# Scan states of a head pair: stored without zero blocks, and each head's states and queries multiplied in their own corner of the array

## The chip, the cores and the metric

The kernel runs on one core of one Trainium2 chip. The metric is the device time of one execution in microseconds (us), as the median of several runs. The engines named below are PE (TensorE, the matrix array), PEld (its weight loads), DVE (VectorE), ACT (ScalarE), POOL (GpSimd) and SP (which issues most DMAs).

## The reference, cut to what matters

Two trunk layers work on 256 context tokens and 1024 latent tokens of width 1024. Each has a mixing part and an MLP. The mixing part has four groups of four heads (HGRN2, mLSTM, retention, GLA). Each group runs a forward and a backward chunkwise scan and sums the two.

```python
def step(S, inp):                       # chunk_linear: HGRN2, retention, GLA
    qc, kc, vc, ac = inp
    b = jnp.cumsum(ac, axis=-2)
...
    b_last = b[..., -1:, :]
    o = (jnp.einsum('bhts,bhsv->bhtv', attn, vc)
         + jnp.einsum('bhtk,bhkv->bhtv', qc * jnp.exp(b), S))
    S_new = (jnp.exp(b_last[..., 0, :])[..., None] * S
             + jnp.einsum('bhsk,bhsv->bhkv', kc * jnp.exp(b_last - b), vc))
    return S_new, o
```

A state S has dk rows (64 for HGRN2 and retention, 32 for GLA) and dv = 64 columns for each head. The change touches the second term of o (queries times state) and the place where S_new is kept. The mLSTM scan has a form of its own (chunk_mlstm), whose states the kernel keeps in another buffer.

## The kernel before, in words

All 1280 tokens lie as 10 chunks of 128 columns; channels lie on the partitions. One layer runs: norm and modulation; the mixers; the output projection; the MLP. All dense products are made of three matmuls each (L294 to L296, or L632 to L634 for values, L601 for GLA's values and the small gates), with operands split into a high and a low part in a type that PE takes in one pass. The scans' matmuls are plain f32, and the trace shows each of them as two matmul records (two passes), each with its own weight load.

In `mixers` the scans run one after another: GLA (four heads at once), HGRN2 pair 0 and 1, mLSTM pair 0 and 1, retention pair 0 and 1. Each scan is a generator; the class `Fill` lets dense products of the projections and gates run between its steps, so that PE has work while DVE and ACT prepare the scan's operands. The order that results in each engine's queue is made when the program is built: a scheduler moves instructions that are ready ahead of others, so an instruction may stand far from its neighbours in the source.

A scan (`mix_vec` for GLA and HGRN2, `mix_rt` for retention) has two parts.

- The states. For 4, 4 and 2 chunks the keys are transposed, `state_update` (L818) multiplies keys and values of each head into one PSUM bank, and `evac_states` copies the results into the buffer ST on ACT. ST has 128 columns for each chunk and direction: rows of the pair's first head have their state in columns 0 to 63 and zeros in 64 to 127, rows of the second head the other way round. To get the zeros each bank is copied twice with a 0/1 column as scale (`hsel`, L1196). mLSTM calls the same function without a scale (L1193). Then `chain` runs the recurrence over the chunks on DVE: eight dependent instructions for each direction (L799 and L803), 16 for each scan.
- The outputs. For up to 4 chunks the queries are scaled (L919, L1038), the attention matrix is built over levels of halved blocks (L976 to L1032, on DVE, ACT and PE), `direct` makes its innermost two diagonals (L932 to L959, with a small matmul on L956), and `out_chunks` sums everything in a PSUM bank: for each direction one matmul of ST with the queries (L831), then for each head one matmul of the values with the attention matrix (L834), which fills half of the array's columns, at column 0 or 64. `finish` (L703 to L710) normalises.

The buffers of the scans come from `Heap`, a next-fit allocator; the size of ST's buffer is in `SIZES`.

Of the kernel before, what the change touches and what calls it, by code (L numbers as in the profile page):

```python
# [9 lines left out]
AF = mybir.ActivationFunctionType  # L10
# [6 lines left out]
NC = 10  # L17
# [180 lines left out]
class K:  # L198
# [346 lines left out]
        self.late = (tb, r)  # L545


    SIZES = {"raw": NC * 48, "V": NC * 256, "V65": NC * 260, "S": NC * 256, "S65": NC * 130}

    def get(self, S, name):  # L550
        if name not in S:
# [269 lines left out]

    def out_chunks(self, chunks, pair, qd, ST, at, V, kt):

        nc = self.nc
        ps = self.bank(self.obank.next())
        r0, kd, vh = pair
        for i, c in enumerate(chunks):
            o = ps[:, 128 * i:128 * i + 128]
            ds = [d for d in range(2) if (c, d) not in ((0, 0), (1, 1))]
            for j, d in enumerate(ds):  # L830
                nc.tensor.matmul(o, lhsT=ST[r0:r0 + kd, c, d, :], rhs=qd[d](c)[r0:r0 + kd, :], start=(j == 0), stop=False,  # L831
                                 tile_position=(r0, 0))
            for h in range(2):
                nc.tensor.matmul(o[64 * h:64 * h + 64, :], lhsT=V[:, c, vh + h, :], rhs=at(vh + h, c), start=False, stop=True,  # L834
                                 tile_position=(0, 64 * h))
        self.finish(kt, ps[:, 0:128 * len(chunks)], chunks[0], len(chunks))


    def mix_vec(self, S, kind):
        nc, hp = self.nc, self.heap  # L840
# [21 lines left out]
        for d in range(2):  # L862
# [3 lines left out]
            nc.vector.tensor_tensor(rs[d][:, :, far], t[:, :, 0], t[:, :, 1], op=ALU.add)  # L866
            nc.scalar.activation(et[d], t, AF.Exp, scale=esc)
            nc.scalar.activation(dc[d], rs[d][:, :, far], AF.Exp, scale=esc)
        ST = self.get(S, "S")(NC, 2, 128)
        gone = [S[x] for x in (("Q", "B0", "B1") + (("G0", "G1") if hg else ("K",)))]  # L870
        gone2 = [S[x] for x in (("S",) if hg else ("S", "V"))]

        for g0, g1 in ((0, 4), (4, 8), (8, 10)):
            n = 128 * (g1 - g0)
            sl = slice(128 * g0, 128 * g1)
            kk = [hp.alloc(n) for _ in range(2)]
            kno = [hp.alloc(n) for _ in range(2)]
            for d in range(2):
                kd = self.v(kk[d], 2 * (g1 - g0), 64)
                ref = rs[d].rearrange("p a b -> p (a b)")[:, 2 * g0:2 * g1].unsqueeze(2).to_broadcast([128, 2 * (g1 - g0), 64])  # L880
                src = (G[d] if hg else B[d])[:, sl].rearrange("p (a b) -> p a b", b=64)
                if hg:
                    nc.vector.tensor_tensor(kd, src, ref, op=ALU.add)
                else:
                    nc.vector.tensor_tensor(kd, ref, src, op=ALU.subtract)
                kf = self.v(kk[d], n)
                nc.scalar.activation(kf, kf, AF.Exp, scale=esc)
                if not hg:
                    nc.vector.tensor_tensor(kf, kf, Kx[:, sl], op=ALU.mult)
                bk = self.mb.next()  # L890
                T = self.bank(bk).rearrange("p (a b) -> p a b", b=128)
                for i in range(g1 - g0):
                    nc.tensor.transpose(T[:, i, :], kf[:, 128 * i:128 * i + 128], self.ident)
                nc.scalar.activation(self.v(kno[d], n), self.bank(bk)[:, 0:n], AF.Copy)
            bk = self.mb.next()
            for d in range(2):
                kn = self.v(kno[d], g1 - g0, 128)
                for i, c in enumerate(range(g0, g1)):
                    f = self.feeds(c, d)
                    if f is None:  # L900
                        continue
                    ps = self.state_update(c, d, kn[:, i, :], V, heads, ST, bk, d * 4 + i, 64)
            self.evac_states(bk, ST, g0, g1, 64, 4, hs)
            hp.free(*kk, *kno)
            yield (g1 - g0) * (220 + 220 * nh)
        self.chain(ST, lambda c, d: dc[d][:, c:c + 1])
# [3 lines left out]
        for g0 in range(first, NC, step):  # L910
# [139 lines left out]
            hp.free(*qo, ato, cto)  # L1050
            skip = 128 * (g0 if g0 == first and first else 0)
            hp.free_head(skip + n, *gone)
            hp.free_head(2 * (skip + n), *gone2)
            yield m * (430 + 436 * nh)
        hp.free(sm, *gone, *gone2)

    def mgroup(self, nh):

# [59 lines left out]
    def mix_rt(self, S):  # L1118
# [1 line left out]
        heads = [(0, 64, 2 * p), (64, 64, 2 * p + 1)]  # L1120
        V = self.v(S["V"], NC, 4, 64)
        Q, Kx = self.v(S["Q"], NT), self.v(S["K"], NT)
        ST = self.get(S, "S")(NC, 2, 128)
        for g0, g1 in ((0, 4), (4, 8), (8, 10)):
            m = g1 - g0
            n = 128 * m
            bk = self.mb.next()
            for i in range(m):
                nc.tensor.transpose(self.bank(bk)[:, 128 * i:128 * i + 128],
                                    Kx[:, 128 * (g0 + i):128 * (g0 + i) + 128], self.ident)  # L1130
            kno = [hp.alloc(n) for _ in range(2)]
            src = self.bank(bk)[:, 0:n].rearrange("p (c h k) -> p c h k", h=2, k=64)
            for d in range(2):
                sc = self.rtK[:, d, 2 * p:2 * p + 2].unsqueeze(1).unsqueeze(3).to_broadcast([128, m, 2, 64])
                nc.vector.tensor_tensor(self.v(kno[d], n).rearrange("p (c h k) -> p c h k", h=2, k=64), src, sc, op=ALU.mult)
            bk = self.mb.next()
            for d in range(2):
                kn = self.v(kno[d], m, 128)
                for i, c in enumerate(range(g0, g1)):
                    if self.feeds(c, d) is not None:  # L1140
                        self.state_update(c, d, kn[:, i, :], V, heads, ST, bk, d * 4 + i, 64)
            self.evac_states(bk, ST, g0, g1, 64, 4, self.hsel[:, 2:4])
            hp.free(*kno)
            yield m * 900
        self.chain(ST, lambda c, d: self.rtd[:, 8 + 2 * d + p:9 + 2 * d + p])
        first = 0 if l == 0 else 2
        for g0 in range(first, NC, 4):
# [21 lines left out]
            hp.free(*qo, ato)  # L1169
            n += 128 * (first if g0 == first else 0)  # L1170
            hp.free_head(n, S["Q"], S["K"])
            hp.free_head(2 * n, S["S"])
            yield m * 1750
        hp.free(S["S"], S["Q"], S["K"])

    def evac_states(self, bk, ST, g0, g1, w, per, sel=None):

        nc = self.nc
        for d in range(2):
            runs = []  # L1180
            for i, c in enumerate(range(g0, g1)):
                f = self.feeds(c, d)
                if f is None:
                    continue
                if runs and f - c == runs[-1][2] - runs[-1][1] and i == runs[-1][0] + runs[-1][3]:
                    runs[-1][3] += 1
                else:
                    runs.append([i, c, f, 1])
            for i, c, f, m in runs:
                o = (d * per + i) * w  # L1190
                src = self.bank(bk)[:, o:o + m * w].rearrange("p (c v) -> p c v", v=w)
                if sel is None:
                    nc.scalar.activation(ST[:, f:f + m, d, :], src, AF.Copy)  # L1193
                else:
                    for e in range(2):
                        nc.scalar.activation(ST[:, f:f + m, d, 64 * e:64 * e + 64], src, AF.Copy, scale=sel[:, e:e + 1])  # L1196


    def ml_rows(self, sp):
# [541 lines left out]
```

## Time and profile before

| | |
|---|---|
| median of 3 runs | 3275.53 us (3268.72 to 3275.95) |
| profiled execution | 3272.16 us, of which its span is 3270.4 us |
| PE busy | 3189.2 us, 98% of the span |
| DVE, ACT, POOL busy | 2098.0, 1285.5, 11.5 us |
| mean granted TensorE clock | 0.992 of full speed |

The span goes from the first to the last instruction; 1.8 us of the execution's time lie outside it. Busy PE means that some matmul was in the array or on its way through it; matmuls are pipelined, so the time that one costs is read from the distance between starts and not from the length of a record.

### The profile page before, as it was taken

To read this page: it belongs to the slowest core of one execution; us is meant where nothing else is said; L and a number is where in the kernel's file an instruction comes from. 1 tells how busy PE (TensorE), PEld (TensorE's weight loads), DVE (VectorE), ACT (ScalarE), POOL (GpSimd) and SP (SyncE) were. 2 spreads that over 40 slices of the span, in tenths; PEclk is the share of its full clock that TensorE was granted. 3 is DMA by queue.
4 is the path that set the end of the run, shared out by engine and by line. 5 is a ranking of instruction groups with operands and counts; after the bars stand their busy time and mean duration, and the time that the engine had idled before them with its cause. 6 is when DMAs were issued, how large, how long until landed. Compare 5 with 4: busy or idle time off the path is not lost.

```text
span 3270.4 us, 52561 instructions
## 1 busy us (share of the span) xinstructions
PE 3189.2 (98%) x20681; PEld 2612.7 (80%) x20681; DVE 2098.0 (64%) x4333; ACT 1285.5 (39%) x2665; POOL 11.5 (0%) x42
## 2 busy tenths in 40 slices
PE   7999999999999999999999999999999999999998
PEld 4787788877888888888888677788778888888887
DVE  4778887776588845454545586876756555555546
ACT  4666564546332121212122575764544322222222
POOL 0000000000000000000000000000000000000000
PEclk9999899999999999999999999999999999999999
DMA  5115565345157511111111222333324111111111
GB/s 208 60 60 178 180 187 195 117 135 183 57 164 232 161 39 39 39 39 39 39 39 40 78 66 71 118 108 115 94 71 149 58 48 49 46 52 46 52 49 65
DMA packets 181953, 308.20 MB, mean 94 GB/s; under 512 B 21880, under 2 KB 51240, under 8 KB 181448
## 3 DMA queue, kind: packets, MB, share of 16 engines
q1 hardware_dynamic: 180376, 303.02, 28.7%
q8 instruction: 162, 2.65, 0.3%
q10 hardware_dynamic: 1296, 1.81, 0.2%
q14 instruction: 87, 0.71, 0.1%
q0 software_dynamic: 32, 0.01, 0.0%
HBM read 259.11 MB, written 45.65 MB: 93 GB/s over the span
## 4 chain that ended last, share of the span: by engine, by line
PE 84%; DVE 6%; DMA 5%; ACT 3%; issue 1%; SPq 0%; DVEq 0%; ACTq 0%
PE psum L294 22%; PE psum L295 22%; PE psum L296 22%; PE psum L831 2%; PE psum L601 2%; PE psum L632 1%; PE psum L834 1%; PE psum L818 1%; PE psum L634 1%; PE psum L633 1%; PE psum L1019 1%; PE psum L706 1%; DMA ph<-w_adaR 1%; PE psum L1358 1%; DVE px L991 1%
## 5 line engine op out<-in xcount | busy, mean ns | idle before, releaser
L526 DVE SCALAR_TENSOR_TENSOR x<-psum,st,x 128x512 f32<-128x512 f32 (+1 forms) x648 | 440.4, 689 | 204.3 <-PE psum L296 203.8
L282 ACT ACTIVATE pc<-st 128x512 fp32r<-128x512 f32 x256 | 161.3, 632 | 853.5 <-PE psum L295 841.3
L295 PE MATMUL psum<-pc,pc 128*128 128x512 f32 (+1 forms) x1296 | 477.1, 368 | 5.0 <-DVE pc L506 5.0
L294 PE MATMUL psum<-pc,pc 128*128 128x512 f32 (+1 forms) x1296 | 476.3, 368 | 0.0
L296 PE MATMUL psum<-pc,pc 128*128 128x512 f32 (+1 forms) x1296 | 474.9, 366 | 0.0
L294 PE MATMUL psum<-Hhi,pc 128*128 128x512 f32 (+1 forms) x1280 | 471.1, 368 | 1.6 <-ACT pc L282 1.5
L295 PE MATMUL psum<-Hlo,pc 128*128 128x512 f32 (+1 forms) x1280 | 472.0, 369 | 0.1
L296 PE MATMUL psum<-Hhi,pc 128*128 128x512 f32 (+1 forms) x1280 | 470.5, 368 | 0.0
L294 PE MATMUL psum<-Hhi,pw 128*128 128x512 f32 (+1 forms) x1192 | 450.8, 378 | 8.3 <-ACT pw L282 3.9
L296 PE MATMUL psum<-Hhi,pw 128*128 128x512 f32 (+1 forms) x1192 | 447.5, 376 | 0.6 <-DVE pw L283 0.6
L295 PE MATMUL psum<-Hlo,pw 128*128 128x512 f32 (+1 forms) x1192 | 446.5, 375 | 0.0
L505 DVE TENSOR_TENSOR st<-st 128x256 f32<-128x256 f32 (+1 forms) x160 | 101.8, 636 | 301.5 <-ACT pc L504 300.8
L295 PEld LDWEIGHTS psum<-pc,pc 128*128 128x128 f32 x1296 | 245.1, 189 | 47.0 <-DVE pc L506 5.5
L294 PEld LDWEIGHTS psum<-pc,pc 128*128 128x128 f32 x1296 | 245.1, 189 | 44.2 <-DVE x L526 1.3
L296 PEld LDWEIGHTS psum<-pc,pc 128*128 128x128 f32 x1296 | 244.7, 189 | 43.0 <-issue 2.7
L294 PEld LDWEIGHTS psum<-Hhi,pc 128*128 128x128 f32 x1280 | 241.3, 189 | 43.3 <-ACT pc L282 2.4
L295 PEld LDWEIGHTS psum<-Hlo,pc 128*128 128x128 f32 x1280 | 241.3, 189 | 40.9 <-issue 0.5
L283 DVE TENSOR_TENSOR pc<-st,pc 128x512 fp32r<-128x512 f32 x256 | 175.6, 689 | 153.3 <-ACT pc L282 133.4
L296 PEld LDWEIGHTS psum<-Hhi,pc 128*128 128x128 f32 x1280 | 241.1, 188 | 41.0 <-DVE pc L283 0.6
L294 PEld LDWEIGHTS psum<-Hhi,pw 128*128 128x128 f32 x1192 | 227.3, 191 | 54.4 <-issue 9.6
L296 PEld LDWEIGHTS psum<-Hhi,pw 128*128 128x128 f32 x1192 | 227.2, 191 | 39.4 <-issue 2.6
L295 PEld LDWEIGHTS psum<-Hlo,pw 128*128 128x128 f32 x1192 | 227.6, 191 | 37.2 <-issue 2.2
(401 smaller groups left out, 4868.6 us busy)
## 6 DMA issues: line engine op xcount, KB each, us to landing
st<-w_ff SPq DMA_DIRECT2D x256, 256.0 KB
ph<-w_adaR SPq DMA_DIRECT2D x128, 256.0 KB
st<-w_inT SPq DMA_DIRECT2D x96, 256.0 KB
st<-w_adaR SPq DMA_DIRECT2D x74, 256.0 KB
pc<-w_adaR SPq DMA_DIRECT2D x54, 256.0 KB
st<-w_out SPq DMA_DIRECT2D x50, 256.0 KB
d_z<-st SPq DMA_DIRECT2D x40, 256.0 KB
ps<-w_ada SPq DMA_DIRECT2D x32, 256.0 KB
```

Source lines behind the costliest of these rows:

```text
L282: nc.scalar.activation(hi, raw, AF.Copy)
L283: (eng or nc.vector).tensor_tensor(lo, raw, F(hi), op=ALU.subtract)
L294: t.matmul(out, lhsT=w[0], rhs=m[0], start=first, stop=False)
L295: t.matmul(out, lhsT=w[0], rhs=m[1], start=False, stop=False)
L296: t.matmul(out, lhsT=w[1], rhs=m[0], start=False, stop=last)
L505: nc.vector.tensor_tensor(r, r, r, op=ALU.mult)
L526: nc.vector.scalar_tensor_tensor(x, ps, self.mod[:, l, 40 + o, j:j + 1], x, op0=ALU.mult, op1=ALU.add)
L601: t.matmul(ps[:, 0:304], lhsT=h[a], rhs=u[b], start=(k + i == 0), stop=(k == NK - 1 and i == 2))
L632: t.matmul(ps[:, e, :], lhsT=h[0], rhs=u[0], start=(k == 0), stop=False)
L633: t.matmul(ps[:, e, :], lhsT=h[0], rhs=u[1], start=False, stop=False)
L634: t.matmul(ps[:, e, :], lhsT=h[1], rhs=u[0], start=False, stop=(k == NK - 1))
L831: nc.tensor.matmul(o, lhsT=ST[r0:r0 + kd, c, d, :], rhs=qd[d](c)[r0:r0 + kd, :], start=(j == 0), stop=False, tile_position=(r0, 0))
```

## The change

`ST` has 64 columns for each chunk and direction in place of 128: every head's state stands in its own rows, without the zero block. `evac_states` has lost its scale and copies each run of chunks once, for all scans. `out_chunks` makes two matmuls for each direction: head h takes its rows of ST as weights and its rows of the queries, and writes output partitions 64h to 64h + 63, so it stands at row a and column 64h of the array. The buffer of ST is half as large, and what is freed at a time is halved with it.

```diff
-    SIZES = {"raw": NC * 48, "V": NC * 256, "V65": NC * 260, "S": NC * 256, "S65": NC * 130}
+    SIZES = {"raw": NC * 48, "V": NC * 256, "V65": NC * 260, "S": NC * 128, "S65": NC * 130}
@@ out_chunks
             for j, d in enumerate(ds):
-                nc.tensor.matmul(o, lhsT=ST[r0:r0 + kd, c, d, :], rhs=qd[d](c)[r0:r0 + kd, :], start=(j == 0), stop=False,
-                                 tile_position=(r0, 0))
+                for h in range(2):
+                    a = r0 + kd // 2 * h
+                    nc.tensor.matmul(o[64 * h:64 * h + 64, :], lhsT=ST[a:a + kd // 2, c, d, :], rhs=qd[d](c)[a:a + kd // 2, :],
+                                     start=(j == 0), stop=False, tile_position=(a, 64 * h))
@@ mix_vec (mix_rt alike)
-        ST = self.get(S, "S")(NC, 2, 128)
+        ST = self.get(S, "S")(NC, 2, 64)
...
-            self.evac_states(bk, ST, g0, g1, 64, 4, hs)
+            self.evac_states(bk, ST, g0, g1, 64, 4)
...
-            hp.free_head(2 * (skip + n), *gone2)
+            for x, k in gone2:
+                hp.free_head(k * (skip + n), x)
@@ evac_states
-    def evac_states(self, bk, ST, g0, g1, w, per, sel=None):
+    def evac_states(self, bk, ST, g0, g1, w, per):
...
-                if sel is None:
-                    nc.scalar.activation(ST[:, f:f + m, d, :], src, AF.Copy)
-                else:
-                    for e in range(2):
-                        nc.scalar.activation(ST[:, f:f + m, d, 64 * e:64 * e + 64], src, AF.Copy, scale=sel[:, e:e + 1])
+                nc.scalar.activation(ST[:, f:f + m, d, :], src, AF.Copy)
```

The counts of instructions change on two engines: PE has 408 state matmuls in place of 204, and ACT has 112 state copies in place of 192 (160 with a scale and 32 of mLSTM). In the changed kernel L831 is L833, L834 is L836, L956 is L958, L1000 and L1019 are L1002 and L1021, L894 and L887 are L896 and L889, L985 is L987, and L1193 and L1196 are L1195.

The scheduler's order moves too. Three places follow. The first is PE's queue in layer 0 at the end of the first output step of HGRN2 pair 0, where `direct` and `out_chunks` follow each other. Before:

```order
L296 MATMUL psum<-Hhi,pw_0_252 128x512
L294 MATMUL psum<-Hhi,pw_0_252 128x512
L295 MATMUL psum<-Hlo,pw_0_252 128x512
L296 MATMUL psum<-Hhi,pw_0_252 128x512
L956 MATMUL psum<-st,px_0_693 128x2 x8
L294 MATMUL psum<-Hhi,pw_0_252 128x256
L295 MATMUL psum<-Hlo,pw_0_252 128x256
L834 MATMUL psum<-px_0_693,ph_0_256 64x128 x2
L831 MATMUL psum<-px_0_693,ph_0_256 128x128
L834 MATMUL psum<-px_0_693,ph_0_256 64x128 x2
L831 MATMUL psum<-px_0_693,ph_0_256 128x128 x2
L834 MATMUL psum<-px_0_693,ph_0_256 64x128 x2
```

And in the changed kernel at the same place:

```order
L294 MATMUL psum<-Hhi,pw_0_252 128x512
L295 MATMUL psum<-Hlo,pw_0_252 128x512
L296 MATMUL psum<-Hhi,pw_0_252 128x512
L294 MATMUL psum<-Hhi,pw_0_252 128x512
L295 MATMUL psum<-Hlo,pw_0_252 128x512
L296 MATMUL psum<-Hhi,pw_0_252 128x512
L958 MATMUL psum<-st,px_0_693 128x2 x4
L836 MATMUL psum<-px_0_693,ph_0_256 64x128 x2
L833 MATMUL psum<-px_0_693,ph_0_256 64x128 x2
L836 MATMUL psum<-px_0_693,ph_0_256 64x128 x2
L833 MATMUL psum<-px_0_693,ph_0_256 64x128 x4
L836 MATMUL psum<-px_0_693,ph_0_256 64x128 x2
```

The eight small matmuls of `direct` stood together before; now the first four stand 13 dense matmuls of 512 columns ahead of the last four (six of the 13 are shown), and the two dense matmuls that stood between `direct` and `out_chunks` are gone from there.

The second is PE's queue a little earlier, at the head of that same output step, where the first state matmul of the pair was moved ahead, among dense matmuls. Before:

```order
L1000 MATMUL psum<-px_0_693 64x64 x14
L296 MATMUL psum<-Hhi,pw_0_252 128x512
L831 MATMUL psum<-px_0_693,ph_0_256 128x128
L1019 MATMUL psum<-px_0_693 32x2x32 x16
L294 MATMUL psum<-Hhi,pw_0_252 128x512
```

And in the changed kernel:

```order
L294 MATMUL psum<-Hhi,pw_0_252 128x512
L833 MATMUL psum<-px_0_693,ph_0_256 64x128 x2
L295 MATMUL psum<-Hlo,pw_0_252 128x512
L296 MATMUL psum<-Hhi,pw_0_252 128x512
L1021 MATMUL psum<-px_0_693 32x2x32 x16
```

The state matmul still stands alone there, now as two, with dense matmuls on both of its sides.

The third is ACT's queue during the states of HGRN2 pair 0 of layer 0, from the first state copies to the scaling of the queries (L918, now L920). Before:

```order
L1196 ACTIVATE ph_0_256<-psum,st 128x4x64 x2
L1196 ACTIVATE ph_0_256<-psum,st 128x64 x6
L894 ACTIVATE px_0_693<-psum 128x512
L887 ACTIVATE px_0_693<-px_0_693 128x512
L887 ACTIVATE px_0_693<-px_0_693 128x256 x2
L308 ACTIVATE st<-st 128x512
L894 ACTIVATE px_0_693<-psum 128x512
L894 ACTIVATE px_0_693<-psum 128x256 x2
L918 ACTIVATE px_0_693<-ph_0_256 128x512
L1196 ACTIVATE ph_0_256<-psum,st 128x4x64 x4
L1196 ACTIVATE ph_0_256<-psum,st 128x64 x2
L1196 ACTIVATE ph_0_256<-psum,st 128x2x64 x2
```

And in the changed kernel:

```order
L1195 ACTIVATE ph_0_256<-psum 128x64
L708 ACTIVATE st<-st 128x128
L896 ACTIVATE px_0_693<-psum 128x512 x2
L308 ACTIVATE st<-st 128x512
L889 ACTIVATE px_0_693<-px_0_693 128x256 x2
L309 ACTIVATE st<-st 128x512
L1195 ACTIVATE ph_0_256<-psum 128x4x64 x2
L896 ACTIVATE px_0_693<-psum 128x256 x2
L920 ACTIVATE px_0_693<-ph_0_256 128x512
L1195 ACTIVATE ph_0_256<-psum 128x64
L1195 ACTIVATE ph_0_256<-psum 128x2x64
```

The second batch of state copies, eight instructions before, is four now, in two pieces around the first scaling of the queries.

## Rows read from the trace of the kernel before

**Rows 1.** mixers by window: length, then PE, PEld, DVE, ACT busy

```profile
90.00:780.00 690.00, 664.87 (x6037) 534.86 (x6036) 548.53 (x1418) 386.38 (x912) 1.54 (x14) 0.98 0.43 137
1870.00:2456.00 586.00, 573.62 (x5129) 460.11 (x5129) 420.90 (x953) 344.71 (x775) 1.61 (x14) 1.00 0.29 93
```

**Rows 2.** PE timeline at 337 us: start, length, engine, line, [wait <- releaser]

```profile
337.83 1.87 PE L956 MATMUL psum<-st,px 128*128 128x2 f32 x8 [3.85 <-DVE px L935]
341.15 0.58 PE L294 MATMUL psum<-Hhi,pw 128*128 128x256 f32 x1 [1.45 <-DVE st L651]
```

**Rows 3.** three windows at half clock: after POOL's column stands PEclk

```profile
307.10:310.50 3.40, 3.40 (x10) 2.66 (x9) 3.27 (x8) 2.08 (x5) 0.00 (x0) 0.51 0.54 200
334.50:351.50 17.00, 12.21 (x55) 8.46 (x57) 12.41 (x27) 7.70 (x16) 0.00 (x0) 0.50 0.24 76
679.20:686.00 6.80, 4.66 (x33) 4.25 (x32) 5.77 (x16) 3.16 (x11) 0.00 (x0) 0.50 0.75 235
```

**Rows 4.** PE timeline at 303 us

```profile
303.20 0.49 PE L831 MATMUL psum<-px,ph 128*128 128x128 f32 x2 [0.73 <-DVE px L1038]
305.80 0.65 PE L1019 MATMUL psum<-px 128*32 128x64 f32 x32 [2.10 <-ACT px L985]
```

**Rows 5.** DVE timeline ahead of that

```profile
303.67 0.34 DVE L803 SCALAR_TENSOR_TENSOR ph<-ph 128x128 f32<-128x128 f32 x1
303.93 0.41 DVE L981 TENSOR_TENSOR px<-px 128x256 f32<-128x256 f32 x1
```

**Rows 6.** PE timeline through one HGRN2 output step

```profile
390.62 0.44 PE L834 MATMUL psum<-px,ph 128*64 128x128 f32 x4 [0.21 <-ACT px L1044]
390.99 0.49 PE L831 MATMUL psum<-ph 128*128 128x128 f32 x2
391.31 0.39 PE L831 MATMUL psum<-px,ph 128*128 128x128 f32 x2
391.63 0.44 PE L834 MATMUL psum<-px,ph 128*64 128x128 f32 x4
...
394.62 0.40 PE L294 MATMUL psum<-Hhi,pw 128*128 128x512 f32 x1
394.86 0.40 PE L295 MATMUL psum<-Hlo,pw 128*128 128x512 f32 x1
...
397.23 0.67 PE L831 MATMUL psum<-px,ph 128*128 128x128 f32 x4
397.66 0.48 PE L296 MATMUL psum<-Hhi,pw 128*128 128x512 f32 x1
```

**Rows 7.** PE timeline, retention's keys times queries (L1163)

```profile
748.51 1.71 PE L1163 MATMUL psum<-ph 64*128 64x128 f32 x16
750.15 0.49 PE L831 MATMUL psum<-px 128*128 128x128 f32 x2
```

**Rows 8.** DVE groups by shape: xcount | busy us, mean ns | idle

```profile
L803 DVE SCALAR_TENSOR_TENSOR ph<-ph 128x128 f32<-128x128 f32 x32 | 11.1, 347 | 0.7 <-ACT ph L1196 0.4
...
L803 DVE SCALAR_TENSOR_TENSOR px<-px,ph 128x65 f32<-128x65 f32 x32 | 9.0, 281 | 4.4 <-ACT px L1193 4.4
```

**Rows 9.** groups of ACT by line

```profile
L1196 ACT ACTIVATE px<-psum,st 128x64 f32<-128x64 f32 (+2 forms) x96 | 28.5, 398 | 21.9 <-PE psum L818 21.8
...
L1196 ACT ACTIVATE ph<-psum,st 128x64 f32<-128x64 f32 (+2 forms) x64 | 18.9, 401 | 1.5 <-PE psum L818 1.4
```

**Rows 10.** ACT timeline, states of HGRN2 pair 0

```profile
290.15 2.07 ACT L1196 ACTIVATE ph<-psum,st 128x256 f32<-128x256 f32 x8
...
296.30 2.50 ACT L1196 ACTIVATE ph<-psum,st 128x256 f32<-128x256 f32 x8 [0.30 <-PE psum L818]
```

**Rows 11.** DVE and ACT timeline after the second group of L956

```profile
339.74 0.44 DVE L959 COPY_PREDICATED px<-st,psum 128x256 f32<-128x256 int32 x1 [1.36 <-PE psum L956]
...
340.21 1.69 ACT L1044 ACTIVATE px<-px 32x256 f32<-32x256 f32 x4 [2.37 <-DVE px L959]
```

**Rows 12.** PE's waits in layer 1's mixers: who for whom, us, times, longest

```profile
PE psum L818 <- ACT px L894: 2.4, 1, 2.4
```

More of the change, by code (lines that the diff above doesn't have):

```diff
@@ L868, in mix_vec @@
             nc.scalar.activation(dc[d], rs[d][:, :, far], AF.Exp, scale=esc)
-        ST = self.get(S, "S")(NC, 2, 128)
+        ST = self.get(S, "S")(NC, 2, 64)
         gone = [S[x] for x in (("Q", "B0", "B1") + (("G0", "G1") if hg else ("K",)))]
-        gone2 = [S[x] for x in (("S",) if hg else ("S", "V"))]
+        gone2 = [(S[x], 1 if x == "S" else 2) for x in (("S",) if hg else ("S", "V"))]
         for g0, g1 in ((0, 4), (4, 8), (8, 10)):
@@ L1052, in mix_vec @@
             hp.free_head(skip + n, *gone)
-            hp.free_head(2 * (skip + n), *gone2)
+            for x, k in gone2:
+                hp.free_head(k * (skip + n), x)
             yield m * (430 + 436 * nh)
-        hp.free(sm, *gone, *gone2)
+        hp.free(sm, *gone, *(x for x, _ in gone2))
     def mgroup(self, nh):
@@ L1122, in mix_rt @@
         Q, Kx = self.v(S["Q"], NT), self.v(S["K"], NT)
-        ST = self.get(S, "S")(NC, 2, 128)
+        ST = self.get(S, "S")(NC, 2, 64)
         for g0, g1 in ((0, 4), (4, 8), (8, 10)):
@@ L1141, in mix_rt @@
                         self.state_update(c, d, kn[:, i, :], V, heads, ST, bk, d * 4 + i, 64)
-            self.evac_states(bk, ST, g0, g1, 64, 4, self.hsel[:, 2:4])
+            self.evac_states(bk, ST, g0, g1, 64, 4)
             hp.free(*kno)
@@ L1171, in mix_rt @@
             hp.free_head(n, S["Q"], S["K"])
-            hp.free_head(2 * n, S["S"])
+            hp.free_head(n, S["S"])
             yield m * 1750
         hp.free(S["S"], S["Q"], S["K"])
-    def evac_states(self, bk, ST, g0, g1, w, per, sel=None):
+    def evac_states(self, bk, ST, g0, g1, w, per):
         nc = self.nc
```

## The prediction

> **What bounds the kernel now.** I read the table first: PE is busy for 98% of the span, so a saving counts only where it takes work out of PE's queue or shortens a wait of PE. Then the windows of the two mixer stretches, the only ones that the change touches [rows 1]: PE is busy for 664.9 of 690.0 us and 573.6 of 586.0, so its waits there add up to 25.1 + 12.4 = 37.5 us. DVE is busy for 79% and 72% of them, ACT for 56% and 59%: both mostly follow PE, and less work for them is worth at most those 37.5 us and what the clock loses after them. Next I read where PE waits. The dearest place is the end of HGRN2 pair 0's first output step in layer 0: 3.85 us for DVE between the two groups of L956, then 1.45 us before a dense matmul [rows 2]. With it goes the clock: from 334.5 to 351.5 us the granted clock is 0.50, which of TensorE's levels is 1.2 GHz and not 2.4. PE was busy for 12.2 us there, which at full clock would be about 6.1, so that stretch costs some 6.1 us; the two shorter ones cost 1.7 and 2.3 by the same halving [rows 3]. The shortest follows a pair of waits that ends the states of HGRN2 pair 0: 0.73 us for L1038 and 2.10 for L985 [rows 4]. Ahead of them DVE works without a break, and a step of the recurrence (L803) stands right ahead of L981, whose result L985 takes [rows 5]. These two places are where the change can pay.
>
> **The state matmuls on PE.** In one output step the rhythm is plain [rows 6]. A group of four state records among dense matmuls takes 397.66 - 397.23 = 0.43 us, 0.107 each. The same four between two value groups take 391.63 - 390.99 = 0.64, so 0.21 us more goes to the change of layout: emptying the array and a first weight load that nothing hides. The value group takes 390.99 - 390.62 = 0.37 us for four records. Its two heads stand in different column halves; if they run side by side it streams for 2 x 0.107 = 0.215, and its change of layout costs 0.155, less since half as many columns are loaded.
>
> The new group has eight records, two heads by four passes. If the heads run side by side as those of the values do, it takes 0.43 + 0.155 = 0.585 between value groups, 0.055 less than now. But the old layout used all columns and was that of the dense matmuls; the new one is not, so a group that stands alone among dense matmuls, as at the second place of the order shown, now pays the change into it and the change back: 0.43 + 0.155 + 0.21 = 0.795, which is 0.365 more. I counted changes of layout over PE's whole order. Before there are 833, of which 486 lead into a layout that loads all columns, 234 into one with half of them, 113 into a quarter. After there are 863: 403, 347 and 113. That makes -83 x 0.21 + 113 x 0.155 = -17.4 + 17.5 = **+0.1 us**. What a group saves beside values is eaten by the 18 groups of HGRN2 and retention that stand alone among dense matmuls. From below, with every one of 118 groups between values, it would be -118 x 0.055 = -6.5; from above, 18 x 0.365 = +6.6 with no gain elsewhere.
>
> Do the heads run side by side? No row shows this layout: two heads in different rows and different columns that write the same PSUM bank. The value heads share a bank, but take the same rows [rows 6]. Retention's 16 passes (L1163) are two heads in different rows and different banks: the whole group takes 750.15 - 748.51 = 1.64 us, where 16 x 0.107 + 0.21 = 1.92 would be one after the other, so they overlap as far as neighbours in the queue allow [rows 7]. The new heads are neighbours and share neither rows nor columns, so I take full overlap. The other end is none: 204 new matmuls, each two passes, come on top, 408 x 0.107 = +43.7 us.
>
> The Trainium skill speaks against me here: TensorEngine Tiling (Array Packing), Restrictions and Gotchas, says that different row tiles cannot use one PSUM bank at the same time; by that the sum would be the +43.7 us. The Trainium skill's page PSUM — Partial Sum Buffer, in its part on bank collisions, narrows this to one bank in the same group of 32 partitions, and the two heads write different halves; by that the sum stays +0.1. No run here shows either yet.
>
> **DVE and ACT.** The recurrence has 16 instructions in each of ten scans, 160 in all. At 128 columns one takes 347 ns, at mLSTM's 65 columns 281 [rows 8]: 0.066 us less each, 1.06 for a scan, 10.6 in all. ACT loses 80 of 160 copies, half of 28.5 + 18.9 us, so 23.7 [rows 9]; for HGRN2 pair 0 that is half of 2.07 + 2.50, so 2.3 us [rows 10]. Nearly everywhere this is hidden: PE has dense matmuls while the states are made. It shows where DVE runs without a break up to PE's wait, at 303 us, so I take **-1.1 us** there, off 2.83. Bounds: 0, if the scheduler's new neighbours fill the room, and -2.8 - 1.7, if the wait and the half-clock stretch after it go. ACT's share I take as hidden, since the wait ends on DVE's L981 through L985; its cover is that DVE chain.
>
> **The new order.** At the first place shown, 13 dense matmuls now stand between the groups of `direct`. A dense matmul of 512 columns takes 394.86 - 394.62 = 0.24 us [rows 6]; 13 give 3.1 us, so the 3.85 us wait shrinks to about 0.8. In return nothing dense stands between the second group and the values, and PE must sit through DVE's copy (L959) and ACT's four copies (L1044): from 339.74 to 340.21 + 1.69 = 341.90, about 2.2 us [rows 11], where it waited 1.45. Together 5.3 becomes 3.0: **-2.3 us**. The half-clock stretch of 17.0 us followed a wait of 3.85. What is left is like the pair 0.73 and 2.10, after which a stretch at half clock came too, but a shorter one. I put it at that of 679 us, 2.3 us in place of 6.1: **-3.8 us**, between 0 and -6.1.
>
> Elsewhere the order takes cover away: at the first GLA step of layer 1 the dense work between the second group of `direct` and the values goes from 2.6 to 0.3 us (counted as above). By the 2.2 us that the copies need, that is a new wait of **+1.9 us**, between 0 and +1.9 + 2.3 with a half-clock stretch. A single wait of 2.4 us in this layer had none after it: the clock of its window is 1.00 [rows 1, 12].
>
> Smaller buffers change addresses and so which instructions wait for a buffer's old readers; I count that at nothing, since no PE wait in the rows is one of those. DMAs are as many as before.
>
> **The sum.** 3272.2 (the profiled execution, 3.4 under the median of three runs) + 0.1 - 1.1 - 2.3 - 3.8 + 1.9 = 3267.0; I say **3267 us**.
>
> **Rivals.**
> - *The heads run one after the other.* Place: every L833 group. For it: no row shows two row groups writing one bank at once. Against it: both halves of the layout overlap when taken singly [rows 6, 7]. Price +43.7 on 3272.2, so 3316 us; it is slower from the point where more than a quarter of the passes (9.8 of 43.7 us) fail to overlap.
> - *The waits of layer 0 go altogether.* DVE and ACT get ahead at 303 us and at 337 us: -2.8 - 1.7 there, -5.3 - 6.1 here, +0.1: 3256 us. For it: DVE's chain is shorter just before. Against it: the copies before the values have no cover in the new order.
> - *The change does nothing for time.* The gains at 337 us are not had, since the waits only change places and the half-clock stretch stays, and layer 1's new wait comes with a stretch of its own: 3272.2 + 0.1 + 1.9 + 2.3 = 3276.5.
>
> **How the numbers follow.** The forecast gets 0.58, the waits gone 0.18, nothing 0.15, heads in turn 0.09. About 0.3% (9.8 us) is what a measurement can tell from no change. Under 3262 lies most of the second rival and a sixth of the forecast: faster 0.27. Over 3282 lie the serial heads and a little of the third: slower 0.12. Same is 0.61. The range takes in the second and third rival with some room for a scheduler's chance: 3252 to 3285; the serial heads stay outside. The forecast's own range is 3259 to 3275.
>
> **What would show it.** In the profile after: L833 groups between values at about 0.59 us with the heads' records some ns apart (right), or near 1.07 (serial heads). Groups alone among dense matmuls near 0.8 us. The recurrence at 281 ns. Waits of about 0.8 and 2.2 us at the end of HGRN2 pair 0's first step, a half-clock stretch well under 17 us, and no more than 1.8 us of wait at its head. The prediction is wrong if PE's busy time in the mixers rises by tens of us, or if new waits with half-clock stretches turn up at places where the order lost its cover.

## The result and the profile after

The changed kernel takes 3313.8 us (median of 4 runs, 3308.26 to 3316.68) where the kernel before took 3275.74 beside it (4 runs, 3268.72 to 3286.57): ratio 1.0100, 95% interval 1.0081 to 1.0119. It is slower, and above the range that I gave. The profiled execution took 3308.26 us with a span of 3306.5; before it was 3272.16 and 3270.4.

First the page of the changed kernel: span, then busy time by engine.

```profile
span 3306.5 us, 53270 instructions
...
PE 3208.3 (97%) x21089; PEld 2612.0 (79%) x21089; DVE 2088.2 (63%) x4333; ACT 1260.5 (38%) x2585; POOL 11.6 (0%) x42
```

PE is idle for 3306.5 - 3208.3 = 98.2 us; before it was 3270.4 - 3189.2 = 81.2. DVE and ACT have less to do, as the change intends, and PE waits 17.0 us more. The other half is the clock. These are windows over the changed kernel, the two mixer stretches [rows 1] and then seven of its fourteen stretches at half clock [rows 3], with the sum over all fourteen; columns as in [rows 1].

```profile
90.00:793.00 703.00, 668.09 (x6250) 530.47 (x6249) 541.11 (x1413) 373.13 (x868) 1.59 (x14) 0.98 0.42 134
1881.00:2490.00 609.00, 589.91 (x5340) 465.62 (x5339) 416.40 (x957) 334.35 (x740) 1.66 (x14) 0.97 0.28 90
...
339.70:343.10 3.40, 3.40 (x26) 2.61 (x16) 3.40 (x8) 1.04 (x2) 0.00 (x0) 0.51 0.80 230
353.40:360.20 6.80, 6.78 (x43) 4.47 (x44) 3.37 (x10) 2.46 (x5) 0.00 (x0) 0.50 0.58 193
551.40:561.60 10.20, 7.18 (x45) 6.57 (x46) 7.62 (x24) 3.91 (x9) 0.00 (x0) 0.50 0.66 166
...
1838.20:1845.00 6.80, 5.25 (x12) 2.14 (x15) 5.50 (x8) 4.86 (x11) 3.76 (x3) 0.50 0.64 210
1920.10:1926.90 6.80, 5.80 (x73) 5.51 (x74) 3.83 (x11) 3.75 (x13) 0.00 (x0) 0.50 0.14 39
1985.00:2002.10 17.10, 17.10 (x121) 11.36 (x121) 3.27 (x7) 4.72 (x10) 0.00 (x0) 0.50 0.26 82
2107.80:2111.20 3.40, 3.40 (x38) 2.73 (x32) 3.40 (x8) 2.76 (x7) 0.00 (x0) 0.51 0.45 154
...
sum 85.70, PE 73.19 PEld 54.23 DVE 53.25 ACT 31.08 POOL 3.76; mean PE 5.23 PEld 3.87 DVE 3.80 ACT 2.22 POOL 0.27
```

PE was busy for 73.2 us at half clock, so it lost about half of that, 36.6 us. The same sum over the seven stretches of before is 35.65 us, so 17.8 lost. That is +18.8, and with the +17.0 of idle time 35.8 of the 36.1 us by which the span grew. What PE executes, taken at full clock, changed by 0.3 us. In the mixers PE now waits 34.9 us in layer 0 and 19.1 in layer 1, where it waited 25.1 and 12.4; and layer 1's mixers, where the mean clock before was 1.00, now lose 14.9 us at half clock.

The new products themselves are as forecast. PE's timeline through one HGRN2 output step of the changed kernel (L836 values, L833 states), and a state group alone among dense matmuls:

```profile
402.08 0.44 PE L836 MATMUL psum<-px,ph 128*64 128x128 f32 x4
402.45 0.65 PE L833 MATMUL psum<-ph 64*64 64x128 f32 x8
403.03 0.44 PE L836 MATMUL psum<-px,ph 128*64 128x128 f32 x4
...
409.08 0.28 PE L632 MATMUL psum<-pw,Hhi 128*128 128x256 f32 x1
409.29 0.65 PE L833 MATMUL psum<-px,ph 64*64 64x128 f32 x8
409.87 0.39 PE L633 MATMUL psum<-pw,Hhi 128*128 128x256 f32 x1
410.10 0.28 PE L634 MATMUL psum<-pw,Hlo 128*128 128x256 f32 x1
```

Eight records take 403.03 - 402.45 = 0.58 us, where four took 0.64 [rows 6]: the heads run side by side. Taken one by one, the records of the two heads start 6 or 7 ns apart in 406 of the kernel's 408 pairs. Alone among dense matmuls, 410.10 - 409.08 = 1.02 less two dense matmuls of 256 columns (0.12 each, half of the 0.24 for 512 [rows 6]) is 0.78. A step of the recurrence fell from about 347 to 280 ns [rows 8], and 112 copies, the 32 of mLSTM among them, take 25.6 us where the 160 alone took 47.4 [rows 9]:

```profile
L799 DVE SCALAR_TENSOR_TENSOR ph<-ph 128x64 f32<-128x64 f32 x32 | 9.0, 280 | 1.4 <-ACT ph L1195 1.2
...
L1195 ACT ACTIVATE px<-psum 128x195 f32<-128x195 f32 (+3 forms) x72 | 16.6, 291 | 41.2 <-PE psum L818 41.1
L1195 ACT ACTIVATE ph<-psum 128x64 f32<-128x64 f32 (+2 forms) x40 | 9.0, 293 | 8.7 <-PE psum L818 8.6
```

So every instruction got as cheap as it should, and the kernel got slower in between. PE's timeline shows where (first the head of HGRN2 pair 0's first output step [rows 4], where no wait is left, and its end [rows 2]; then the last output step of HGRN2 pair 1; then, in layer 1, a wait ahead of its mixers and the first GLA step):

```profile
316.33 0.44 PE L833 MATMUL psum<-px,ph 64*64 64x128 f32 x4
...
317.36 0.65 PE L1021 MATMUL psum<-px 128*32 128x64 f32 x32
...
339.31 0.74 PE L1021 MATMUL psum<-px 128*32 128x64 f32 x32 [3.38 <-DVE px L993]
350.11 1.05 PE L958 MATMUL psum<-st,px 128*128 128x2 f32 x8 [1.98 <-DVE px L937]
353.42 0.70 PE L836 MATMUL psum<-px,ph 128*64 128x128 f32 x4 [2.25 <-ACT px L1046]
...
550.10 0.43 PE L1021 MATMUL psum<-px 128*32 128x64 f32 x16 [1.27 <-DVE px L993]
553.52 0.65 PE L1021 MATMUL psum<-px 128*32 128x64 f32 x16 [2.98 <-DVE px L993]
...
1839.41 0.62 PE L601 MATMUL psum<-pw,Hhi 128*128 128x304 f32 x1 [4.25 <-DVE pw L592]
...
1979.04 0.39 PE L632 MATMUL psum<-pw,Hhi 128*128 128x256 f32 x1 [1.56 <-DVE st L742]
1984.88 0.53 PE L633 MATMUL psum<-pw,Hhi 128*128 128x256 f32 x1 [1.97 <-DVE pw L283]
```

None of the waits stands before an instruction of the change. L1021 is a level of the attention, L632 and L633 are dense work that should fill PE's waits and now waits itself: for a bank that L742 has to empty and for weights that L283 has to split, both late in DVE's queue.

### The profile page after: what moved, and what is told of

Same layout as the page of the kernel before. It is cut to its first block, busy times and chain, and to the rows that moved or that the text cites. A ratio compares the mean times of both kernels' runs of the same rounds, so it can differ in the third digit from the quotient of the medians.

```text
span 3306.5 us, 53270 instructions
## 1 busy us (share of the span) xinstructions
PE 3208.3 (97%) x21089; PEld 2612.0 (79%) x21089; DVE 2088.2 (63%) x4333; ACT 1260.5 (38%) x2585; POOL 11.6 (0%) x42
## 4 chain that ended last, share of the span: by engine, by line
PE 80%; DVE 9%; DMA 6%; ACT 3%; issue 1%; SPq 0%; DVEq 0%; ACTq 0%
PE psum L294 21%; PE psum L295 21%; PE psum L296 21%; PE psum L833 2%; PE psum L601 2%; PE psum L632 1%; PE psum L836 1%; PE psum L633 1%; PE psum L634 1%; PE psum L818 1%; DMA ph<-w_adaR 1%; PE psum L1021 1%; DMA px<-d_u 1%; PE psum L1357 1%; PE psum L706 1%
## 5 line engine op out<-in xcount | busy, mean ns | idle before, releaser
L283 DVE TENSOR_TENSOR pc<-st,pc 128x512 fp32r<-128x512 f32 x256 | 175.6, 690 | 153.3 <-ACT pc L282 133.4
```

What stands on the lines that cost most here:

```text
L283: (eng or nc.vector).tensor_tensor(lo, raw, F(hi), op=ALU.subtract)
```

## The experiments

The theories at the start. **1, the order**: the build writes each engine's order anew, and the loss is in that order. Counted by the fewest instructions that must be moved to turn one order into the other, the change moves 2,627 of 17,327 on PE, 673 of 4,061 on DVE and 469 of 2,593 on ACT. **2, the work**: the doubled matmuls or the changes of layout cost it. **3, the addresses**: the smaller state buffer shifts other buffers, and they are waited for.

The results first, so that the runs can be read against each other. Idle is span less PE's busy time, half-clock half of PE's busy time in the windows at half clock, rest the span less both; each from the one profiled execution of that kernel. Executions of one kernel differ: before, beside e9, took 3274.3 to 3291.3 us, and its mean granted clock lay between 0.987 and 0.992. So the clock column gives the mean over all executions of the kernel, and over those of before beside it.

| kernel | ratio to before, 95% interval | span | idle | half-clock | rest | clock: kernel, before |
|---|---|---|---|---|---|---|
| before | 1 | 3270.4 | 81.2 | 17.8 | 3171.4 | - |
| after | 1.0100 (1.0081 to 1.0119) | 3306.5 | 98.2 | 36.6 | 3171.7 | 0.9852, not listed |
| e1 all work, order of before | 1.0012 (1.0002 to 1.0022) | 3276.4 | 83.8 | 20.0 | 3172.6 | 0.9894, 0.9905 |
| e2 all work, old addresses | 1.0045 (1.0029 to 1.0061) | 3284.8 | 84.2 | 24.2 | 3176.4 | 0.9886, 0.9905 |
| e3 corners alone | 1.0000 (0.9989 to 1.0012) | 3271.3 | 80.1 | 19.8 | 3171.4 | 0.9915, 0.9905 |
| e4 states alone | 1.0124 (1.0102 to 1.0145) | 3317.8 | 100.9 | 43.7 | 3173.2 | 0.9828, 0.9905 |
| e5 all work, order of e3 | 1.0003 (0.9992 to 1.0014) | 3274.0 | 85.4 | 16.0 | 3172.6 | 0.9915, 0.9909 |
| e6 before, order of e2 | 1.0146 (1.0129 to 1.0162) | 3328.5 | 101.3 | 51.5 | 3175.7 | 0.9842, 0.9909 |
| e7 after, order of e4 | 1.0120 (1.0101 to 1.0138) | 3318.2 | 103.4 | 42.0 | 3172.8 | 0.9850, 0.9909 |
| e8 before, longer buffer | 1.0007 (0.9997 to 1.0016) | 3279.6 | 81.3 | 27.1 | 3171.2 | 0.9902, 0.9909 |
| e9 after, waits filled | 1.0080 (1.0065 to 1.0096) | 3312.9 | 82.6 | 37.9 | 3192.4 | 0.9908, 0.9904 |
| e10 e1, waits filled | 0.9994 (0.9983 to 1.0005) | 3273.8 | 71.5 | 13.4 | 3188.9 | 0.9948, 0.9904 |
| e11 before, waits filled | 0.9996 (0.9987 to 1.0005) | 3274.2 | 71.7 | 15.0 | 3187.5 | 0.9944, 0.9904 |
| e12 chain alone | 1.0036 (1.0024 to 1.0049) | 3298.5 | 89.7 | 35.2 | 3173.6 | 0.9894, 0.9899 |
| e13 copies alone | 1.0010 (1.0001 to 1.0020) | 3286.0 | 85.1 | 26.4 | 3174.5 | 0.9911, 0.9899 |

**e1, the old order.** A table of the wanted order is laid over the built program as a chain of order-only links on each engine:

```diff
+        row = [by[e][j] for j in idx]
+        for a, b in zip(row, row[1:]):
+            tc.add_manual_dep(b, a.name, after, reason="order")
-        ST = self.get(S, "S")(NC, 2, 64)
+        ST = self.get(S, "S")(NC, 2, 128)[:, :, :, 0:64]
```

> All of the change's work (64-column states, one copy instead of two, two corner matmuls instead of one), but every engine's instructions in the order that the kernel before has them (the second corner matmul right behind the first, the single copy where the first of the two stood), and the state buffer at the addresses of before. Theory 1, the order: the loss is in the order that the build writes, not in the work; the time is that of before less about 1 us (the shorter chain of states): 3268 to 3277 us, idle time of TensorE and half-clock stretches as before (25 us and 10 us of loss in the mixers of layer 0, 12 us and none in those of layer 1). Theory 2, the work: the doubled matmuls or their changes of layout cost it; the time stays at 3305 to 3315 us with the old order too. Theory 3, the addresses of the smaller state buffer: as theory 1 here, told apart by the next run.

The same work is back at 1.0012, 0.12% above before where I had expected 1 us below it. Theory 2 falls: the doubled matmuls are all in it. Order and addresses are both those of before here, so e1 does not tell theory 1 from theory 3. In layer 1 the waits at L632 and L633 are one of 0.46 us, and no half-clock stretch follows.

**e2, the old addresses**, order left to the build.

```diff
-    SIZES = {... "S": NC * 128, ...}
+    SIZES = {... "S": NC * 256, ...}
```

> The changed kernel with the state buffer as large as before and its states at the old places in it (a gap of 64 columns behind each), so that no other buffer moves; the order is left to the build. Theory 3, addresses: the new waits come from buffers that lie elsewhere; 3268 to 3277 us. Theory 1, the order: the build still writes another order than before (about one instruction in seven on TensorE stands elsewhere), so the time differs from before by some 10 to 45 us, 3280 to 3320 us, with waits at other places than the changed kernel has them. Theory 2: 3305 to 3315 us.

1.0045, which is the number of neither theory 2 nor theory 3, and lies in the range of theory 1: with every other buffer where it was, new waits come all the same, but less than half of the loss. It has its own 17.1 us stretch at half clock, at 1967.6 us. Of the 14.4 us by which its profiled span is above before, 3.0 are idle, 6.4 half-clock and 5.0 rest; those 5.0 stay unexplained.

**e3 and e4, each part alone.**

```diff
 e3, on the kernel before
-                nc.tensor.matmul(o, lhsT=ST[r0:r0 + kd, c, d, :], ...
+                for h in range(2):
+                    a = r0 + kd // 2 * h
+                    nc.tensor.matmul(o[64 * h:64 * h + 64, :], lhsT=ST[a:a + kd // 2, c, d, 64 * h:64 * h + 64], ...
 e4, on the kernel after
+                nc.tensor.matmul(o, lhsT=ST[r0:r0 + kd, max(c, 2), :, :].rearrange("p d v -> p (d v)"), ...
```

> The kernel before with its 128-column states and two copies, but each state product split in two corner matmuls (64 columns of a head's states, that head's rows). Addresses and copies are as before; the order is left to the build and about one TensorE instruction in ten moves. Theory 2 with the matmuls as the cost: 3305 to 3315 us. Theory 1: the work itself adds 0.1 us, the rest is the order's; nothing fixes its sign, 3260 to 3320 us, and the difference to before lies in waits and half-clock stretches and not in the stretches where TensorE runs through. If the copies and the chain are what moves the order for the worse, it is within 5 us of before.

> The changed kernel's states (64 columns, one copy, chain of 64, small buffer) with one matmul for each direction as before; the stationary 128 columns are both directions' states of a chunk, so that the sums are not the reference's, at the same count and shape of matmuls as before. The order is left to the build (about one TensorE instruction in seven moves). Theory 2 with the matmuls as the cost: 3268 to 3277 us, since they are gone. Theory 1: off from before by 10 to 45 us, 3280 to 3320 us, with the difference in waits and half-clock stretches.

The part with the new matmuls costs nothing, the part without them costs 1.2%. But e4 does a little more than take work away: its products read both directions' states of a chunk, and those of chunks 0 and 1 read chunk 2's (`max(c, 2)`), so they hang on other steps of the chain than in any other kernel here. How much of the 1.2% comes from that was not tried.

**e5 and e7, the work of one with the order of another.** The edit is the table of e1, with the order of e3 and of e4.

> All of the change's work (states of 64 columns, single copies, chain of 64, corners), state buffer at the old places, every engine in the order that the build wrote for the corners alone. Theory 1, the order sets the time: as the corners alone in their own order, ratio 0.998 to 1.002, that is 3270 to 3285 us beside a before of 3275 to 3279. Theory 2', the shorter states and copies themselves cost the time (since the states alone were 1.2% slower and the corners alone the same): 1.004 to 1.012.

> The changed kernel, all of its work and its small buffer, every engine in the order that the build wrote for the states alone (e4, ratio 1.0124), the second corner matmul behind the first. Theory 1: ratio 1.010 to 1.015 with long half-clock stretches in the mixers of layer 0 where that kernel has them (356, 564, 598 us), not where the changed kernel has them. Theory 2': as the changed kernel, with its own waits, 1.008 to 1.012; what tells them apart here is where the waits stand: at 550, 1920 and 1985 us if they belong to the work, at 356, 564, 598 and 2370 us if they belong to the order.

Both times follow the order: 1.0003 beside e3's 1.0000, 1.0120 beside e4's 1.0124. So do most of the waits. PE's timeline in layer 0, first e4, then e7:

```profile
536.62 0.39 PE L632 MATMUL psum<-pw,Hhi 128*128 128x256 f32 x1 [1.87 <-ACT px L760]
...
563.11 0.43 PE L1019 MATMUL psum<-px 128*32 128x64 f32 x16 [2.44 <-DVE px L991]
```

```profile
536.59 0.58 PE L632 MATMUL psum<-pw,Hhi 128*128 128x256 f32 x1 [1.87 <-ACT px L760]
...
564.10 0.66 PE L1021 MATMUL psum<-px 128*32 128x64 f32 x16 [2.45 <-DVE px L993]
```

The wait of 1.87 us at 536 us is in neither before nor after; it came over with the order. (L1019 of e4 is L1021 here.) Of the half-clock stretches named beforehand, those at 356, 564 and 2370 us of e4 stand in e7 at 359, 564 and 2363; that at 598 does not, and one of the changed kernel's, at 1920, does, at 1936.

**e6, the reverse**: the kernel before with PE, ACT and SP in e2's order, the table laid over those three engines alone.

> The kernel before, not a bit of the change in its work or its buffers; TensorE, ScalarE and the transfers' queue in the order that the build wrote for the changed kernel with old addresses (the second copy right behind the first), VectorE left to the build. Theory 1: the time goes with the order, ratio 1.003 to 1.008 (that kernel had 1.0045; the longer copies and chain add to it, VectorE's order can take from it). Theory 2': the work of before gives the time of before, 0.998 to 1.002.

1.0146, more than e2's 1.0045: the work of before in that order is slower still. That an order can make the old work slow is shown; its size mixes the longer copies and chain with an order of DVE that the build chose for it, and isn't explained further. The changed kernel's own order was not tried on the work of before, and no order of before on the smaller buffer.

**e8, a harmless edit**: `"S": NC * 264` in the kernel before.

> The kernel before with one number changed: the state buffer is 2,640 columns long and not 2,560; no work changes, other buffers lie a little elsewhere. The build moves about 600 of 17,327 TensorE instructions. If the build's order answers to any small change with new waits, the ratio leaves 1 by more than 0.3% either way; if only the change of the work or of its estimated durations does that, it is within 0.2% of 1.

1.0007: not every small edit hurts.

**e12 and e13, the two halves of the states.**

```diff
 e12
     def chain(self, ST, dec):
+        ST = ST[:, :, :, 0:64] if ST.shape[-1] == 128 else ST
 e13
-                    for e in range(2):
-                        nc.scalar.activation(ST[:, f:f + m, d, 64 * e:64 * e + 64], src, AF.Copy, scale=sel[:, e:e + 1])
+                    nc.scalar.activation(ST[:, f:f + m, d, :].rearrange("p c (e v) -> p c e v", e=2),
+                                         src.unsqueeze(2).to_broadcast([128, m, 2, w]), AF.Copy, scale=sel[:, 0:1])
```

> The kernel before with only the chain of states shortened: its 160 steps multiply and add 64 of the 128 columns (the other 64 keep what the copies left, so these states are not the reference's). Order left to the build; about one TensorE instruction in eight moves. Theory 1: any change of a step's length makes the build write another order, whose price has nothing to do with the work: ratio anywhere from 0.997 to 1.012, and off 1 by the waits and half-clock stretches of the mixers. Theory 2' (a shorter chain saves about 1 us): 0.999 to 1.001.

> The kernel before with only the two copies of a state group made one: one instruction of twice the columns, scaled by the first head's mask in both halves (so the states of the second head are not the reference's). Order left to the build. Theory 1: as for the chain alone, 0.997 to 1.012. Theory 2' (80 instructions of ScalarE fewer, which waits for nothing here): 0.999 to 1.001. If the loss of the states alone (e4, 1.0124) comes from one edit, that edit alone gives 1.008 or more, and the other 0.998 to 1.003; if both give under 1.003, it comes from the smaller buffer or from the edits together.

Shortening 160 steps of DVE, and nothing else in the source, makes the kernel 0.36% slower; the copies alone add 0.1%, about what can't be told from none. Neither gives e4's 1.2%, so the rest comes from the smaller buffer, from the edits together or from what e4's products read; which, stays open. What e12 shows is how new waits come about. PE's waits in layer 1's GLA step, in e12:

```profile
1971.81 0.39 PE L632 MATMUL psum<-pw,Hhi 128*128 128x256 f32 x1 [1.07 <-DVE st L742]
1977.64 0.58 PE L633 MATMUL psum<-pw,Hhi 128*128 128x256 f32 x1 [1.97 <-DVE pw L283]
```

It is the pair of the changed kernel, and e2 and e6 have it too, with 1.59 and 1.97 us. In each of the four a half-clock stretch of 17.1 us begins there: at 1985.0 us in the changed kernel, 1967.6 in e2, 1983.0 in e6 and 1977.1 in e12. The kernel before, e1, e3 and e5 have no such stretch, and one wait of 0.45 to 0.49 us in place of the pair. (The profiled execution of e12 is the longest of its seven. Over all of them its mean clock is about that of before, so on average its 0.36% lies more in waits than in half-clock stretches.) DVE's timeline tells why PE waits; first the changed kernel, then e1 with the order of before (L732 is a scan behind which both have this work to do):

```profile
1974.65 1.20 DVE L732 TENSOR_TENSOR_SCAN st<-st 128x512 f32<-128x512 f32 x1
...
1978.32 0.67 DVE L742 TENSOR_TENSOR st<-st,psum 128x512 f32<-128x512 f32 x1
...
1984.14 1.28 DVE L283 TENSOR_TENSOR pw<-st,pw 128x512 fp32r<-128x512 f32 x2
```

```profile
1958.31 1.22 DVE L732 TENSOR_TENSOR_SCAN st<-st 128x512 f32<-128x512 f32 x1
1959.44 0.66 DVE L742 TENSOR_TENSOR st<-st,psum 128x512 f32<-128x512 f32 x1
...
1961.63 0.68 DVE L283 TENSOR_TENSOR pw<-st,pw 128x512 fp32r<-128x512 f32 x1
...
1969.30 0.68 DVE L283 TENSOR_TENSOR pw<-st,pw 128x512 fp32r<-128x512 f32 x1
```

In the old order L742 empties the bank 1.1 us after the scan starts and the first half of the weights is split 3.3 us after. In the new one it takes 3.7 and 9.5 us: six other instructions stand ahead of L742 where there was none, and sixteen ahead of L283 where there were five. PE runs out of dense work, waits 3.5 us, and then works for 17.1 us at half clock, 8.6 us lost: some 12 us at this one place. That the order of DVE's queue is the cause at this place is read from the two timelines; moving these instructions alone was not tried.

**e9 to e11, filling the waits.** Products of constants ahead of the longer waits, into the bank that the waiting matmul overwrites, in an order held fixed.

```diff
+        for _ in range(WARM.get((site, i), 0)):
+            n = min(256, ps.shape[-1])
+            x = self.nc.tensor.matmul(ps[:, 0:n], lhsT=self.ident, rhs=self.m64[:, 0:n], start=True, stop=True)
```

> The changed kernel in its own order, and ahead of ten of TensorE's longer waits (339, 350, 550, 553, 689, 834, 1078, 1839, 1921 and 2107 us in its trace) 2 to 9 products of constants with 256 columns, 44 in all, written to the bank that the waiting matmuls then overwrite; they are meant to end before what TensorE waits for. Theory A: about half of the loss (36.7 us of half-clock loss in this kernel, 17.9 in the kernel before) is the clock that falls behind a wait, so with the waits filled the stretches at 551, 667, 691, 834, 1077, 1838, 1920 and 2107 us go and 12 to 22 us come back: ratio to before 1.003 to 1.007, the stretch at 1985 us (17 us long, behind waits that are not filled) stays. Theory B: the stretches don't hang on these waits, or the products keep the real work back: ratio 1.008 to 1.014.

> All of the change's work with the state buffer at the old places in the order of the kernel before (e1, ratio 1.0012), and 33 products of constants ahead of eight waits of that order (306, 333, 338, 676, 810, 1062, 1823 and 1905 us in the trace of e1). Theory A: the half-clock loss of 20 us there falls by 10 to 18 us: ratio 0.995 to 0.999. Theory B: 1.000 to 1.004.

> The kernel before in its own order with the same 33 products at the same places. Theory A: 10 to 17 us of its 17.9 us half-clock loss come back: ratio 0.9945 to 0.998, which would show that the gain belongs to the filled waits and not to the change; e10 then lies within 0.2% of it. Theory B: 0.999 to 1.003.

The time is a miss for theory A, the clock is not. The changed kernel gains 0.2% at best (1.0080 after 1.0100, and the two intervals overlap); e10 and e11 can't be told from before.

In the profiled execution of e9 the stretches behind the filled waits at 1078, 1839 and 1921 us are gone, but others stand at 2289.4 (13.7 us long) and 2367.9 (10.2), the one at 1985 stayed, and the half-clock loss is 37.9 us, as without the filling. That execution (3314.7 us, clock 0.987) is the longest of five, though. The other four took 3298.5 to 3304.8 us at 0.991 or 0.992, where the four of the changed kernel stand at 0.983 to 0.987. In e10 and e11 the mean clock rises too, from 0.9894 (e1) and 0.9904 (before) to 0.9948 and 0.9944; every execution of e10 is above every one of before beside it.

So filled waits do give the clock back. What they cost is TensorE's own time: against the same kernel without them the rest column grows by 20.7 us in e9, 16.3 in e10 and 16.1 in e11, more than the idle column falls (15.6, 12.3 and 9.5). Fewer products for each wait were not tried. No version here is faster than the kernel before by more than the measurement can tell; the nearest is e10.

## Why the prediction was wrong

**The state matmuls, +0.1: right**, with its working: 0.58 for the 0.585 between values, 0.78 for the 0.795 alone, corners alone at 1.0000, and the rest column within 0.3 us. One after the other, the heads would take about 1.07 us (twice 0.43 and a change of layout of 0.21). The Trainium skill says in TensorEngine Tiling (Array Packing), Restrictions and Gotchas, that different row tiles can't use one PSUM bank at the same time; for these halves the measurement differs, 0.58 us with records 6 or 7 ns apart. The Trainium skill's page PSUM — Partial Sum Buffer, on bank collisions, puts the error down to row tiles that write one bank in the same group of 32 partitions; these heads write different groups, and the trace agrees.

**The serial heads, 3316 us: false**, though the measured time lies next to it, which is chance. Only the rows tell these apart: the loss is between the matmuls, not in them. (The "more than a quarter" of that rival is a slip: 9.8 of 43.7 us is 22%.)

**The shorter chain at 303 us, -1.1: 0 by itself.** With the old neighbours, in e1, PE waits 0.93 + 1.95 = 2.88 us there, where it was 2.83 [rows 4]:

```profile
303.89 0.43 PE L833 MATMUL psum<-px,ph 64*64 64x128 f32 x4 [0.93 <-DVE px L1040]
306.27 0.88 PE L1021 MATMUL psum<-px 128*32 128x64 f32 x32 [1.95 <-ACT px L987]
```

DVE's timeline in e1 shows where the gain went. The chain's steps are shorter, but among them stands L414, which now waits for a transfer; before, DVE had no wait in this stretch:

```profile
302.07 0.69 DVE L414 SCALAR_TENSOR_TENSOR ph<-ph 128x512 f32<-128x512 f32 x1 [0.70 <-DMA ph<-w_adaR]
```

In the changed kernel itself the whole wait at this place is gone (L833 and L1021 at 316 and 317 us above), and the half-clock stretch of 1.7 us after it too. That is my lower bound, -2.8 - 1.7, but the new order brought it and not the chain, which e1 has as well. ACT's copies hidden: right (e1 gains nothing from them).

**The new order, -2.3 - 3.8 + 1.9: the step that failed.** At the end of that step 3.85 and 1.45 [rows 2] became 1.98 and 2.25, so -1.1 and not -2.3, and a wait of 3.38 us for L993 stands ahead of them that I had not looked for. Over the whole step, with the pair's states ahead of it, PE waits 9.6 us where it waited 10.1: the waits changed places, as the third rival had it. Half-clock loss at its end went from 6.1 [rows 3] to (3.40 + 6.78) / 2 = 5.1: -1.0, not -3.8. In layer 1 the wait for the copies that I priced at +1.9 did not come (no wait at L836 there is above 0.3 us); the dense work waits itself, 1.56 + 1.97 and 8.6 of clock, 12 us in place of 1.9 with a bound of 4.2. And all the places that I did not price, since "some room for a scheduler's chance" was to hold them: over the whole kernel +17.0 of idle time and +18.8 of clock, of which 21.6 us lie in the mixers of layer 1 and 12.7 in those of layer 0. I read a few places of an order in which one PE instruction in seven had moved, and put the rest at nothing. What the prediction named as making it wrong, new waits with half-clock stretches where the order lost its cover, is what came.

**Smaller buffers at nothing**: none of the waits shown is for an old reader of a buffer that moved. But with the old addresses e2 has less than half of the loss, so the smaller buffer may have its part, through the order that the build writes for it; no run has the smaller buffer in an order of before, so how large that part is stays open. e1 and e5 show that at the old addresses, in an order that is good, the work is nearly free (1.0012 and 1.0003).

## What to carry to other kernels

Where a build step writes the order, an edit has two prices, that of its instructions and that of a new order, and here the first was about 0.1% at the old addresses (e1). The spread of the second (0 to 1.2% over seven builds from edits of the same few lines) belongs into the range, whatever the edit saves. Hold the order fixed (e1) to learn what the edit itself is worth before judging it, and keep an order that is known to be good. In a stretch where TensorE lives on filler, look at what the filler needs from the other engines (its bank emptied, its weights split) and where that stands in their queues. And before a wait is filled with other products, compare what they cost TensorE with what the clock gives back.

## What the runs showed of the hardware

Two products with different rows, different columns and one PSUM bank, of which they write different halves of the partitions, run side by side: eight records in 0.58 us.

A pair of waits of 1.56 and 1.97 us, 5.8 us apart, was followed by 17.1 us at a granted clock of 0.50. A single wait of 4.25 us, to 1839.4 us, had 6.8 us at half clock, from 1838.2 on. So the length of the wait does not tell the length of the stretch, and what does these runs leave open.

Products of constants in the waits raised the mean granted clock of before from 0.9904 to 0.9944 (e11), and the time stayed (0.9996), since the rest column grew by 16.1 us.
